# Three instead of two k-tile pairs of the first feed-forward product taken through seven block products, in another order of the pairs

## The chip, the core and the metric

The kernel runs on one core of a Trainium2 chip. The core has a matrix engine (TensorE, called PE in the profile), a vector engine (VectorE, DVE), a scalar engine (ScalarE, ACT), GpSimd (POOL) and SyncE (SP), which here issues all the transfers. Each engine takes its instructions in the order in which they stand in the program; engines wait for each other on semaphores. The metric is the device time of one execution in microseconds (us); lower is better.

## What is computed

The reference is a decoder layer in float32 for 256 tokens of width 2048: a gated mixer of two attention branches, a cross-attention, and a SwiGLU feed-forward block, each followed by a layer norm. The change lies in the first product of the feed-forward block, `x @ w_in`:

```python
D_MODEL = 2048
D_FF = -(-8 * D_MODEL // (3 * 256)) * 256      # 5632

def swiglu(x, w_in, w_out):
    g, u = jnp.split(x @ w_in, 2, axis=-1)
    return (jax.nn.silu(g) * u) @ w_out
...
        y = swiglu(x, w_ffn_in[l], w_ffn_out[l])
        x = layer_norm(ALPHA * x + y, ln_g[l, 2], ln_b[l, 2])
```

## The kernel before

Float32 products are made of three matmuls each. An operand is split into `hi` (rounded by ScalarE, L117) and `lo` (the rest, a subtraction on VectorE, L118), and `mm3` adds hi·hi (L268), hi·lo (L269) and lo·hi (L270) in PSUM. So every weight tile that comes from memory costs one activation, one subtraction, and then matmuls. L268 and L270 need only the `hi` half of the weight, L269 needs the `lo` half.

The feed-forward width 5632 is cut into 11 slices of 512 columns, j = 0 to 10. Slice 0 is made by the ordinary `product`. Slices 1 to 10 are ten **passes** of one loop. A pass makes the gate and the up columns of its slice for both halves of the tokens, so four accumulators of 128 tokens by 512 columns (x11, x12, x21, x22: token half, then gate or up). The depth 2048 is 16 k-tiles, taken as 8 pairs c = 0 to 7 (`KC = 2`). A pair can be done in two ways:

- `plain_cell`: for gate and for up one transfer of two weight tiles (512 KB) into a `raw` buffer, one split into an `hl` buffer (128 x 1024 elements), and 12 matmuls; 24 matmuls for the pair.
- `fast_cell`: gate and up times two k-tiles times two token halves form a 2 x 2 block product, done with seven block products instead of eight (Winograd's form of Strassen's scheme), 21 matmuls. The sums of activations it needs are made once ahead of the passes (`fast_acts`, tile `sq`). The sums of weights are made in each pass by VectorE: L914, L915 (tile `tw`), L918, L919 (tile `s`), 128 x 512 each, and then three splits of 128 x 1024 into `hl` and one of 128 x 512 into `s`. Four of the seven products go to PSUM banks of their own (m1, m5, m6, m7, pool `aux`). After the last fast pair of the pass, `sums` joins them into four `stage` tiles (L948 to L952).

At the end of a pass four VectorE additions read the accumulators (L990, L992), ScalarE applies silu (L991), a product is made (L993), and the result is written out to DRAM (`keep`, L196). `turn` reads it back with its tokens turned (four transfers, L181), VectorE transposes it (L187, four instructions), ScalarE and VectorE split it (L188, L190). That is done during the next pass.

Tile's scheduler decides the order of the instructions on each engine. There are five `raw` buffers, four `hl` buffers, one `tw` buffer, two `s` buffers, and 14 buffers `b8`, which hold among others the 4 quads of the input activations, `sq` and the turned results of the slices.

```python
    FAST = (0, 1)
    ORDER = (0, 2, 3, 1, 4, 5, 6, 7)
...
            for i, c in enumerate(ORDER):
                if c in FAST:
                    fast_cell(bk, x2T, sq, FAST.index(c), c, ws, c == FAST[-1])
```

Of the kernel before, what the change touches and what calls it, by code (L numbers as in the profile page):

```python
# [65 lines left out]
def trunk(ctx: ExitStack, tc: tile.TileContext, a, out: bass.AP):  # L66
# [34 lines left out]
    def stage(dtype=F32):  # L101
        return work.tile([P, W], dtype, tag="stage", name=nm("stage"), bufs=4)
# [55 lines left out]
    def to_quad(q, tt, src):  # L158
        p = ps_aux()
        for i in range(4):  # L160
            nc.tensor.transpose(p[:, i * P:(i + 1) * P], src[:, i * P:(i + 1) * P], ident)  # L161
        sl = slice(tt * P, (tt + 1) * P)
        pv = p.rearrange("p (k t) -> p k t", k=4)
        split(q.hi[:, :, sl], q.lo[:, :, sl], pv)
# [206 lines left out]
    for ps in wide(w_in[:, C_QI:C_KI], load_x):  # L371
        t = b8().rearrange("p (h t) -> p h t", h=8)
# [26 lines left out]
    for tt in range(NT):  # L399
# [8 lines left out]
        st = work.tile([P, 6], F32, tag="st1", name=nm("st1"))  # L408
# [448 lines left out]

    FAST = (0, 1)  # L860
    ORDER = (0, 2, 3, 1, 4, 5, 6, 7)

    def fast_acts():

        q = Quad()
        for t, c in enumerate(FAST):
            st = stage()
            a11, a12 = [tok[0][:, (2 * c + i) * P:(2 * c + i + 1) * P] for i in range(2)]
            a21, a22 = [tok[1][:, (2 * c + i) * P:(2 * c + i + 1) * P] for i in range(2)]
            s1, s2, s3, s4 = [st[:, i * P:(i + 1) * P] for i in range(4)]  # L870
            nc.vector.tensor_tensor(s1, a21, a22, op=ALU.add)
            nc.vector.tensor_tensor(s2, s1, a11, op=ALU.subtract)
            nc.vector.tensor_tensor(s3, a11, a21, op=ALU.subtract)
            nc.vector.tensor_tensor(s4, a12, s2, op=ALU.subtract)
            to_quad(q, t, st)
        return q

    class Banks:

# [78 lines left out]
    for j in range(DFF // W):  # L958
        gs = []

        def gate(tt, p):
            g = stage()
            nc.scalar.activation(g, p, AF.Silu)
            gs.append(g)

        q = Quad()
        d = spill()
        if j == 0:
            product(x2T, [wf[:, j * W:(j + 1) * W]], seq=8, stream_seq=3, done=gate)
            side.finish()  # L970
            sq = fast_acts()
            pu = product(x2T, [wf[:, DFF + j * W:DFF + (j + 1) * W]])
            for tt in range(NT):
                nc.vector.tensor_tensor(gs[tt], gs[tt], pu[tt], op=ALU.mult)
                keep(d, tt, gs[tt])
        else:
            ws = [wf[:, j * W:(j + 1) * W], wf[:, DFF + j * W:DFF + (j + 1) * W]]
            bk = Banks(None)
            for i, c in enumerate(ORDER):
                if c in FAST:  # L980
                    fast_cell(bk, x2T, sq, FAST.index(c), c, ws, c == FAST[-1])
                    flush()
                    side.step(1)
                    if c == FAST[-1]:
                        cs = sums(bk)
                else:
                    plain_cell(bk, x2T, c, ws, i == len(ORDER) - 1)
            for tt in range(NT):
                g, u = cs[2 * tt:2 * tt + 2]
                nc.vector.tensor_tensor(g, g, bk.t[f"x{tt + 1}1"], op=ALU.add)  # L990
                nc.scalar.activation(g, g, AF.Silu)  # L991
                nc.vector.tensor_tensor(u, u, bk.t[f"x{tt + 1}2"], op=ALU.add)  # L992
                nc.vector.tensor_tensor(g, g, u, op=ALU.mult)  # L993
                keep(d, tt, g)
        later.append(turn(q, d))
        q.mixed = True
        hT.append(q)
# [33 lines left out]
```

## Time and profile before

| what | value |
|---|---|
| median of 3 runs | 1470.9 us (1468.82 to 1473.25) |
| the profiled execution's own time | 1469.42 us |
| its span, first to last instruction | 1467.3 us |
| PE busy | 98% |
| DVE busy | 71% |
| ACT busy | 48% |
| granted TensorE clock | 0.998 of full speed |
| ten passes of the loop | from about 794 to about 1218 us of the span |

The busy shares are averages over the whole program. The change touches only the ten passes, a little under a third of the span, and what it is worth is read there: which engine has gaps, how long they are, and what ended them.

### The profile page before, as it was taken

What the parts mean: (1) busy time and instruction counts of PE and PEld (TensorE: products, weight loads), DVE (VectorE), ACT (ScalarE), POOL (GpSimd) and SP (SyncE); (2) the same over time, 40 slices, a digit from 0 to 9 for tenths busy, and PEclk for the clock granted to TensorE, in tenths of its full rate; (3) what the DMA queues carried; (4) which work ended last, traced back from release to release, by engine and by line L of the source; (5) the groups of instructions that cost most, each with busy time, mean ns of one, the idle gap of its engine ahead of it and who ended that gap; (6) DMA issues with size and microseconds to landing.
All of it is one profiled execution on the core that took longest, in us unless ns stands there. A gap on an engine that the chain in (4) does not pass through costs nothing.

```text
span 1467.3 us, 17933 instructions
## 1 busy us (share of the span) xinstructions
PE 1444.1 (98%) x6604; PEld 1198.4 (82%) x6604; DVE 1045.3 (71%) x1361; ACT 706.8 (48%) x830; POOL 19.6 (1%) x43
## 2 busy tenths in 40 slices
PE   8999999999999999999989999999999999999997
PEld 6988888888888888888868888888888888888885
DVE  6575986575756666986786888898888886544456
ACT  4554456454534444445644555555455454434341
POOL 0000000000000000000000000000000000000000
PEclk9999999999999999999999999999999999999999
DMA  9884667777667779968535666766776768666662
GB/s 284 194 270 144 198 210 228 227 236 225 214 202 231 219 254 316 231 185 272 177 131 182 206 222 218 242 214 216 229 223 222 243 206 265 191 198 190 197 216 100
DMA packets 197463, 316.60 MB, mean 216 GB/s; under 512 B 18688, under 2 KB 58752, under 8 KB 197376
## 3 DMA queue, kind: packets, MB, share of 16 engines
q1 hardware_dynamic: 197376, 315.47, 69.1%
q8 instruction: 51, 0.84, 0.2%
q14 instruction: 36, 0.29, 0.1%
HBM read 298.65 MB, written 16.78 MB: 215 GB/s over the span
## 4 chain that ended last, share of the span: by engine, by line
PE 91%; DMA 4%; DVE 3%; issue 1%; ACT 0%; POOL 0%; SPq 0%; POOLq 0%; DVEq 0%; ACTq 0%
PE acc L230 20%; PE acc L231 20%; PE acc L229 19%; PE acc L270 8%; PE acc L269 8%; PE acc L268 8%; PE aux L269 2%; PE aux L270 2%; PE aux L268 2%; DMA turn<-spill 1%; DMA raw<-in_w_in 1%; DVE b L751 1%; DVE hl L118 1%; DMA kvg<-in_kv_norm_g 1%; DMA spill<-stage 0%
## 5 line engine op out<-in xcount | busy, mean ns | idle before, releaser
L118 DVE TENSOR_TENSOR hl<-raw,hl 128x1024 fp32r<-128x1024 f32 (+2 forms) x475 | 571.1, 1212 | 272.3 <-ACT hl L117 271.3
L117 ACT ACTIVATE hl<-raw 128x1024 fp32r<-128x1024 f32 (+2 forms) x475 | 496.3, 1052 | 513.0 <-PE acc L231 347.2
L230 PE MATMUL acc<-hl,b 128*128 128x512 f32 (+1 forms) x1272 | 493.8, 388 | 0.7 <-DVE hl L118 0.5
L231 PE MATMUL acc<-hl,b 128*128 128x512 f32 (+1 forms) x1272 | 493.3, 388 | 0.0
L229 PE MATMUL acc<-hl,b 128*128 128x512 f32 (+1 forms) x1272 | 491.3, 389 | 0.7 <-ACT b L117 0.7
L230 PEld LDWEIGHTS acc<-hl,b 128*128 128x128 f32 x1272 | 238.9, 188 | 48.6 <-DVE hl L118 1.5
L229 PEld LDWEIGHTS acc<-hl,b 128*128 128x128 f32 x1272 | 238.8, 188 | 48.4 <-ACT b L117 0.9
L231 PEld LDWEIGHTS acc<-hl,b 128*128 128x128 f32 x1272 | 238.9, 188 | 48.1 <-DVE b L118 0.2
L269 PE MATMUL acc<-hl,b 128*128 128x512 f32 x584 | 227.8, 391 | 0.5 <-DVE hl L118 0.4
L270 PE MATMUL acc<-hl,b 128*128 128x512 f32 x584 | 226.9, 390 | 0.0
L268 PE MATMUL acc<-hl,b 128*128 128x512 f32 x584 | 210.3, 391 | 0.3 <-ACT hl L117 0.2
L269 PEld LDWEIGHTS acc<-hl,b 128*128 128x128 f32 x584 | 109.9, 188 | 25.1 <-DVE hl L118 2.2
L268 PEld LDWEIGHTS acc<-hl,b 128*128 128x128 f32 x584 | 110.0, 189 | 24.2 <-ACT hl L117 1.1
L270 PEld LDWEIGHTS acc<-hl,b 128*128 128x128 f32 x584 | 109.7, 188 | 22.7
L187 DVE STREAM_TRANSPOSE tr<-turn 128x256 f32<-128x256 f32 (+1 forms) x148 | 67.1, 511 | 64.2 <-DMA turn<-spill 64.1
L188 ACT ACTIVATE b<-tr 128x1024 fp32r<-128x1024 f32 (+1 forms) x37 | 37.4, 1014 | 76.9 <-DVE tr L187 75.3
L117 ACT ACTIVATE b<-aux 128x512 fp32r<-128x512 f32 (+1 forms) x50 | 26.7, 545 | 37.0 <-PE aux L161 21.5
L190 DVE TENSOR_TENSOR b<-tr,b 128x1024 fp32r<-128x1024 f32 (+1 forms) x37 | 42.8, 1162 | 1.8 <-ACT b L188 1.4
L117 ACT ACTIVATE hl<-s 128x1024 fp32r<-128x1024 f32 x20 | 21.3, 1063 | 31.0 <-DVE s L919 13.3
L914 DVE TENSOR_TENSOR tw<-raw,raw 128x512 f32<-128x512 f32 x20 | 13.8, 691 | 31.2 <-DMA raw<-in_w_ffn_in 31.1
L118 DVE TENSOR_TENSOR b<-aux,b 128x512 fp32r<-128x512 f32 (+1 forms) x50 | 30.0, 621 | 3.3 <-ACT b L117 3.0
L269 PE MATMUL aux<-hl,b 128*128 128x512 f32 x80 | 31.5, 394 | 0.1
(158 smaller groups left out, 1013.4 us busy)
## 6 DMA issues: line engine op xcount, KB each, us to landing
raw<-in_w_ffn_in SPq DMA_DIRECT2D x176, 512.0 KB, 4.8
raw<-in_w_in SPq DMA_DIRECT2D x143, 512.0 KB, 4.5
raw<-in_w_ffn_out SPq DMA_DIRECT2D x88, 512.0 KB, 4.2
raw<-in_w_out SPq DMA_DIRECT2D x32, 512.0 KB, 6.6
spill<-stage SPq DMA_DIRECT2D x56, 256.0 KB, 2.4
turn<-spill SPq DMA_DIRECT2D x104, 128.0 KB, 3.8
raw<-in_w_o_dsa SPq DMA_DIRECT2D x16, 512.0 KB, 4.6
raw<-in_w_o_moba SPq DMA_DIRECT2D x16, 512.0 KB, 4.0
```

Of the source, the lines that this page charges most:

```text
L117: nc.scalar.activation(hi, src, AF.Copy)
L118: return (eng or nc.vector).tensor_tensor(lo, src, f(hi), op=ALU.subtract)
L187: nc.vector.transpose(tr[:, i, :], v[:, i])
L188: nc.scalar.activation(hi, tr, AF.Copy)
L190: nc.vector.tensor_tensor(lo, tr, f(hi), op=ALU.subtract)
L229: nc.tensor.matmul(o[:, :n], xh, hi[:, kk, :n], start=k == 0, stop=False)
L230: nc.tensor.matmul(o[:, :n], xh, lo[:, kk, :n], start=False, stop=False)
L231: nc.tensor.matmul(o[:, :n], xl, hi[:, kk, :n], start=False, stop=k == kts - 1)
L268: nc.tensor.matmul(o, lh, rh, start=start, stop=False)
L269: nc.tensor.matmul(o, lh, rl, start=False, stop=False)
L270: nc.tensor.matmul(o, ll, rh, start=False, stop=stop)
L751: prev = nc.vector.scalar_tensor_tensor(t, t, scalar, self.rows[row][:, j * W:(j + 1) * W], op0=op0, op1=op1)
```

## The change

`FAST` gets a third pair, so in each pass three pairs go through `fast_cell` and five through `plain_cell`, and `ORDER` puts a plain pair behind each fast one: 0, 3, 1, 4, 2, 5, 6, 7, where it was 0, 2, 3, 1, 4, 5, 6, 7. `sums` runs after pair 2, the fifth in order, where it ran after pair 1, the fourth. `fast_acts` makes the sums of a third pair and needs a second quad, which takes one more of the `b8` buffers through all passes. Lines of the kernel move by two: L914 becomes L916, L919 becomes L921, L993 becomes L995, L187 and below stay.

```diff
-    FAST = (0, 1)
-    ORDER = (0, 2, 3, 1, 4, 5, 6, 7)
+    FAST = (0, 1, 2)
+    ORDER = (0, 3, 1, 4, 2, 5, 6, 7)
 
     def fast_acts():
 
-        q = Quad()
+        qs = []
         for t, c in enumerate(FAST):
+            if t % 2 == 0:
+                qs.append(Quad())
             st = stage()
...
-            to_quad(q, t, st)
-        return q
+            to_quad(qs[-1], t % 2, st)
+        return qs
...
                 if c in FAST:
-                    fast_cell(bk, x2T, sq, FAST.index(c), c, ws, c == FAST[-1])
+                    fast_cell(bk, x2T, sq[FAST.index(c) // 2], FAST.index(c) % 2, c, ws, c == FAST[-1])
```

The scheduler makes a new order of it. Three places on VectorE matter, all in the middle passes. **The first** is the start of a pass's work, from the last products of the pass before (L993) to the transposes of the turned result (L187). Before:

```order
L993 TENSOR_TENSOR stage_7972<-stage_7972,stage_7973 128x512
L993 TENSOR_TENSOR stage_7974<-stage_7974,stage_7975 128x512
L118 TENSOR_TENSOR hl_8186<-raw_8184,hl_8186 128x1024
L118 TENSOR_TENSOR hl_8209<-raw_8207,hl_8209 128x1024
L118 TENSOR_TENSOR hl_8228<-raw_8226,hl_8228 128x1024
L118 TENSOR_TENSOR hl_8245<-raw_8243,hl_8245 128x1024
L914 TENSOR_TENSOR tw_8268<-raw_8262,raw_8260 128x512
L915 TENSOR_TENSOR tw_8268<-raw_8262 128x512
L187 STREAM_TRANSPOSE tr_8201<-turn_8179 128x256 x4
```

And in the changed program (L995 is what L993 was):

```order
L995 TENSOR_TENSOR stage_8064<-stage_8064,stage_8065 128x512
L995 TENSOR_TENSOR stage_8066<-stage_8066,stage_8067 128x512
L118 TENSOR_TENSOR hl_8267<-raw_8265,hl_8267 128x1024
L921 TENSOR_TENSOR s_8296<-raw_8284,s_8296 128x512
L118 TENSOR_TENSOR hl_8288<-raw_8284,hl_8288 128x1024
L118 TENSOR_TENSOR s_8299<-raw_8286,s_8299 128x512
L118 TENSOR_TENSOR hl_8291<-tw_8292,hl_8291 128x1024
L118 TENSOR_TENSOR hl_8295<-s_8296,hl_8295 128x1024
L187 STREAM_TRANSPOSE tr_8259<-turn_8237 128x256 x4
```

Both have four rows of 128x1024 and two of 128x512 between L993 and L187; in the changed program they are the splits of the second fast pair, and the splits of the plain pair behind it stand behind L187. **The second place** follows. It is the last fast pair of the pass, up to the first plain split behind it. Before:

```order
L918 TENSOR_TENSOR s_8272<-raw_8262,tw_8268 128x512
L118 TENSOR_TENSOR hl_8264<-raw_8260,hl_8264 128x1024
L118 TENSOR_TENSOR s_8275<-raw_8262,s_8275 128x512
L919 TENSOR_TENSOR s_8272<-raw_8260,s_8272 128x512
L190 TENSOR_TENSOR b_1190_7796<-tr_8201,b_1190_7796 128x1024
L118 TENSOR_TENSOR hl_8267<-tw_8268,hl_8267 128x1024
L118 TENSOR_TENSOR hl_8271<-s_8272,hl_8271 128x1024
L118 TENSOR_TENSOR hl_8314<-raw_8312,hl_8314 128x1024
```

In the changed program, where it is the third fast pair:

```order
L118 TENSOR_TENSOR hl_8365<-raw_8361,hl_8365 128x1024
L920 TENSOR_TENSOR s_8373<-raw_8363,tw_8369 128x512
L118 TENSOR_TENSOR s_8376<-raw_8363,s_8376 128x512
L118 TENSOR_TENSOR hl_8368<-tw_8369,hl_8368 128x1024
L921 TENSOR_TENSOR s_8373<-raw_8361,s_8373 128x512
L118 TENSOR_TENSOR hl_8372<-s_8373,hl_8372 128x1024
L118 TENSOR_TENSOR hl_8415<-raw_8413,hl_8415 128x1024
```

Before, two rows of 128x1024 stand between the sum L919 and the split of its tile into `hl`; in the changed program the split follows the sum (L921) at once. **The third place** is later in the pass, ahead of the first fast pair of the next pass (L914, L916). Before:

```order
L118 TENSOR_TENSOR hl_8365<-raw_8363,hl_8365 128x1024
L951 TENSOR_TENSOR stage_8304<-stage_8304,aux_8155 128x512
L952 TENSOR_TENSOR stage_8306<-stage_8305,aux_8155 128x512
L118 TENSOR_TENSOR hl_8382<-raw_8380,hl_8382 128x1024
L118 TENSOR_TENSOR hl_8399<-raw_8397,hl_8399 128x1024
L914 TENSOR_TENSOR tw_8468<-raw_8462,raw_8460 128x512
```

In the changed program:

```order
L118 TENSOR_TENSOR hl_8449<-raw_8447,hl_8449 128x1024
L118 TENSOR_TENSOR hl_8466<-raw_8464,hl_8466 128x1024
L952 TENSOR_TENSOR stage_8406<-stage_8405,aux_8217 128x512
L118 TENSOR_TENSOR hl_8483<-raw_8481,hl_8483 128x1024
L953 TENSOR_TENSOR stage_8405<-stage_8405,aux_8213 128x512
L954 TENSOR_TENSOR stage_8407<-stage_8406,aux_8213 128x512
L916 TENSOR_TENSOR tw_8535<-raw_8529,raw_8527 128x512
```

The transfer into the second `raw` tile of L916 (raw_8529) takes the buffer of raw_8447, so it can be issued when the first row here is done; five rows stand between. Before, the second tile (raw_8462) takes the buffer of raw_8380, one row further from L914.

## Rows read from the trace of the kernel before

**Rows 1.** The page: busy time of each engine over the span.

```profile
PE 1444.1 (98%) x6604; PEld 1198.4 (82%) x6604; DVE 1045.3 (71%) x1361; ACT 706.8 (48%) x830; POOL 19.6 (1%) x43
```

**Rows 2.** Busy time by windows: two passes, from one L993 to the next.

```profile
core 0: us, PE busy (x) PEld busy (x) DVE busy (x) ACT busy (x) POOL busy (x), PEclk, DMA share, GB/s
1049.19:1091.43 42.24, 42.24 (x188) 34.91 (x187) 36.20 (x45) 22.21 (x25) 0.00 (x0) 1.00 0.69 224
1091.43:1133.67 42.24, 42.24 (x188) 34.91 (x187) 35.57 (x44) 21.27 (x24) 0.00 (x0) 1.00 0.71 224
```

**Rows 3.** Timeline of PE: first and last of 40 matmuls without a gap.

```profile
start us, us, engine line op out<-in xcount [idle before <-releaser]
1081.40 0.39 PE L270 MATMUL acc<-hl,b 128*128 128x512 f32 x1
...
1090.24 0.39 PE L270 MATMUL acc<-hl,b 128*128 128x512 f32 x1
```

**Rows 4.** Timeline of DVE: from L993 through the second fast pair.

```profile
1091.43 1.29 DVE L993 TENSOR_TENSOR stage<-stage,stage 128x512 f32<-128x512 f32 x2
1092.63 3.58 DVE L118 TENSOR_TENSOR hl<-raw,hl 128x1024 fp32r<-128x1024 f32 x3
1096.56 1.23 DVE L118 TENSOR_TENSOR hl<-raw,hl 128x1024 fp32r<-128x1024 f32 x1 [0.35 <-ACT hl L117]
1098.02 0.69 DVE L914 TENSOR_TENSOR tw<-raw,raw 128x512 f32<-128x512 f32 x1 [0.23 <-DMA raw<-in_w_ffn_in]
1098.63 0.69 DVE L915 TENSOR_TENSOR tw<-raw 128x512 f32<-128x512 f32 x1
1100.67 2.20 DVE L187 STREAM_TRANSPOSE tr<-turn 128x256 f32<-128x256 f32 x4 [1.36 <-DMA turn<-spill]
1102.79 0.66 DVE L918 TENSOR_TENSOR s<-raw,tw 128x512 f32<-128x512 f32 x1
1103.36 1.23 DVE L118 TENSOR_TENSOR hl<-raw,hl 128x1024 fp32r<-128x1024 f32 x1
1104.49 0.69 DVE L118 TENSOR_TENSOR s<-raw,s 128x512 fp32r<-128x512 f32 x1
1105.10 0.69 DVE L919 TENSOR_TENSOR s<-raw,s 128x512 f32<-128x512 f32 x1
1105.70 1.23 DVE L118 TENSOR_TENSOR hl<-tw,hl 128x1024 fp32r<-128x1024 f32 x1
1107.00 1.23 DVE L118 TENSOR_TENSOR hl<-s,hl 128x1024 fp32r<-128x1024 f32 x1
```

**Rows 5.** Timeline of SP at the same place: result out, turned result in.

```profile
1092.14 0.94 SPq L196 DMA_DIRECT2D spill<-stage  x2
1093.88 0.38 SPq L894 DMA_DIRECT2D raw<-in_w_ffn_in  x1
1094.91 1.80 SPq L181 DMA_DIRECT2D turn<-spill  x4
```

**Rows 6.** Timeline of DVE: the earliest pair of L993 and L187 that waits.

```profile
837.18 1.29 DVE L993 TENSOR_TENSOR stage<-stage,stage 128x512 f32<-128x512 f32 x2
...
847.74 2.18 DVE L187 STREAM_TRANSPOSE tr<-turn 128x256 f32<-128x256 f32 x4 [2.74 <-DMA turn<-spill]
```

**Rows 7.** Timeline of ACT: the split of the tile that L919 finishes.

```profile
1105.90 1.06 ACT L117 ACTIVATE hl<-s 128x1024 fp32r<-128x1024 f32 x1 [3.43 <-DVE s L919]
```

**Rows 8.** Timeline of DVE ahead of the next pass's first fast pair.

```profile
1073.89 1.23 DVE L118 TENSOR_TENSOR hl<-raw,hl 128x1024 fp32r<-128x1024 f32 x1
1075.44 1.23 DVE L118 TENSOR_TENSOR hl<-raw,hl 128x1024 fp32r<-128x1024 f32 x1 [0.32 <-ACT hl L117]
1080.02 0.69 DVE L914 TENSOR_TENSOR tw<-raw,raw 128x512 f32<-128x512 f32 x1 [3.35 <-DMA raw<-in_w_ffn_in]
```

**Rows 9.** Waits in all passes (790 to 1216 us): total us, times, longest.

```profile
DVE tw L914 <- DMA raw<-in_w_ffn_in: 31.1, 13, 4.2
DVE hl L118 <- ACT hl L117: 18.1, 31, 1.5
DVE tr L187 <- DMA turn<-spill: 14.8, 8, 2.7
PEld aux L269 <- DVE hl L118: 1.2, 3, 0.6
```

**Rows 10.** Groups by line, 770 to 800 us: the transposes of `fast_acts`.

```profile
L161 PE MATMUL aux<-ident,stage 128*128 128x128 f32 x8 | 1.4, 272 | 0.0
```

## Prediction

> **What bounds the kernel now.** I read the busy shares first [rows 1]: the matrix engine is busy 98% of the span, VectorE 71%. That is an average over stages, so the next view is the ten passes alone. Two of them, cut from one L993 to the next, last 42.24 us each [rows 2]. The reader should see two things there: the matrix engine has no gap in them, and VectorE is busy for 36.2 us of 42.24, far above its average.
>
> How full the matrix engine is must be read from starts, since its rows overlap. Forty matmuls start between 1081.40 and 1090.24 [rows 3], so one takes 8.84 / 39 = 0.2267 us. A pass has 2 fast pairs of 21 and 6 plain ones of 24, 186 matmuls, and 186 x 0.2267 = 42.2 us. That is the pass: the matrix engine sets its length. The list of waits agrees: it waited on VectorE for 1.2 us in all passes together, while VectorE waited 31.1 us for weights, 18.1 us for ScalarE and 14.8 us for the turned result [rows 9]. VectorE's waits cost nothing as long as the matrix engine has work.
>
> [...]
>
> **What the change removes.** Three matmuls per pass: 3 x 0.2267 = 0.68 us, 6.8 us over ten passes. The matrix engine's floor becomes 183 x 0.2267 = 41.5 us per pass.
>
> **What it adds.** Once: four transposes and one more split in `fast_acts`. Eight transposes took 1.4 us of the matrix engine [rows 10], so four cost 0.7 us; the vector work lies in slice 0, an ordinary product with little vector work, and I cost it at nothing (four short sums and a split, under 2 us if nothing covered them).
>
> In each pass a plain pair becomes a fast one. The price of a VectorE row is the distance to the next start where nothing waits: L118 on `s` at 1104.49, L919 at 1105.10, the next at 1105.70, so 0.605 us for 512 columns; L118 at 1103.36 to 1104.49, so 1.13 us for 1024 [rows 4]. A plain pair has two splits of 1024, 2.26 us. A fast one has five rows of 512 and three of 1024, 6.42 us. Added: 4.16 us per pass. ScalarE gets 1.5 us more on 22 busy us [rows 2] and stays far from the bound. No transfer of a pass is added: a fast pair loads the same two 512 KB tiles.
>
> The whole VectorE work of a new pass: 25 rows of 512 (15 of the fast pairs, 4 of `sums`, 6 of the end) at 0.605 = 15.1; 20 of 1024 (10 plain splits, 9 fast ones, L190) at 1.13 = 22.6; four transposes, 1100.67 to 1102.79, 2.1 [rows 4]. Sum 39.8 us. The same count for the pass before (20, 19 and 4) gives 35.7, against 36.2 busy in the window [rows 2], so the method holds.
>
> [...]
>
> So VectorE has 41.5 - 39.8 = 1.7 us per pass in which it may wait. Beyond that it sets the length. This is the step that decides: which of its waits are fixed by the order, and don't shrink when VectorE falls behind?
>
> **First, the turned result.** From the end of the second L993 (VectorE is free at 1092.63) to the first L187 (1100.67) pass 8.04 us [rows 4]. That is the way through memory: the results go out, the turned read starts at 1094.91 [rows 5] and lands when L187 starts. VectorE cannot shorten it, since the clock starts at its own L993. The longest case in the loop is 837.18 + 1.2 to 847.74, 9.4 us [rows 6]. In the changed order the rows between are again four of 1024 and two of 512, 5.73 us, and the next row is L187. So VectorE stands still for 8.04 - 5.73 = 2.3 us there, and the splits of the next plain pair are queued behind it; the matrix engine, through with the second fast pair, waits for them. Before, the same 2.3 us were there (0.35 + 0.23 + 1.36 marked, the rest in short gaps), but VectorE had 6 us to spare. The weight transfer that SP issues between result and turned read waits for the first split behind L995, as it did before [rows 5], so I leave 8.04.
>
> **Second, the last sum of the third fast pair.** Its split stands directly behind it. L919 started at 1105.10, ScalarE could take its tile at 1105.90 for 1.06 us [rows 7], and the subtraction came at 1107.00 [rows 4]: 1.90 us from start to start. Before, a row of 1024 filled most of it. Now only the 0.6 us of L921 itself does: 1.3 us of wait.
>
> **Third, the weights of the next first fast pair.** Their second tile can be fetched when the split of raw_8447 is done. Before, from the end of that buffer's split (1073.89 + 1.23) to L914 at 1080.02 passed 4.9 us [rows 8]. Five rows stand between now, 2 x 1.13 + 3 x 0.605 = 4.1 us, so about 0.9 us of wait (the split's end lies 0.1 behind the next start). Before, the wait was 3.35 there [rows 8]; it shrinks because VectorE is later, not to nothing.
>
> Length of a full new pass: 39.8 + 2.3 + 1.3 + 0.9 = **44.3 us**, 2.1 more than 42.24. The bounds: not under 39.8 + 2.3 = 42.1 if the last two waits vanish in others, and at the other end 46.5 with the 9.4 us of [rows 6] and 0.8 more at the weights.
>
> Not all passes are full. In the changed order five are (slices 2 to 6): 10.5 us; in one of them only four rows follow the freed weight buffer, 0.6 more. In slices 7 and 8 L190 is put off (no `b8` buffer is free; `sq` holds one more): 43.2, so +1.0 each, again 0.6 more in one: 2.6. Slice 1 has no sum directly ahead of its split: 44.3 - 1.3 = 43.0, +0.8. Slice 9 has neither L187 nor L190; VectorE has 36.6 us, and the matrix engine's floor holds: -0.7. Slice 10 gets the postponed L187 and L190; two of these stand ahead of its last fast pair's splits, some 1 us of wait against the floor: +0.3. With the transposes: 10.5 + 0.6 + 2.6 + 0.8 - 0.7 + 0.3 + 0.7 = 14.8 us.
>
> The profiled execution took 1469.42 us (span 1467.3), 1.5 below the median of the runs. 1469.4 + 14.8 = 1484.2; the median lies by as much above as before at most, and I say 1485.
>
> **The rivals.**
>
> - *The matrix engine still sets the pass: faster.* It gains 6.8 - 0.7 = 6.1, so 1463.3. For this VectorE's waits must fit into 1.7 us per pass; the way of the result through memory would have to be under 7.4 us instead of 8.04. For it speaks that 39.8 is under 41.5; against it, that none of the passes with a wait had under 8.0. Chance 0.07.
> - *Only the turned result's wait stays* and the others are hidden behind it, since VectorE catches up where the matrix engine is held: a full pass of 42.1 to 43, others at the floor of 41.5: 1469.4 - 2 to + 6, so 1467 to 1475. Chance 0.19.
> - *More waits than I count.* The late splits hold `hl` buffers, ScalarE waits for these, and the weights come later still: 46.5 us and more per pass, 1469.4 + 10 x 2.5 to 10 x 4, so 1495 to 1509. For it speaks that the changed stretch alternates fast and plain with four `hl` buffers; against it, that I find the buffers free in time when I follow them through the order. Chance 0.10.
> - *Each VectorE row costs its whole duration.* 43.9 + 4.5 = 48.4, +6.2 per pass, about 1520. The starts in [rows 4] speak against it. By the durations in the same rows it is 25 x 0.69 + 20 x 1.23 + 2.1 = 43.9. Chance 0.02. [...]
>
> **How the numbers follow.** My forecast, VectorE sets the pace with these three waits, has 0.62 and gives 1479 to 1491. About 0.3%, 4.4 us, is what a measurement of this kernel can tell from no change. Slower: 0.62 + 0.12 + a sixth of the second rival = 0.77; within: the rest of it, 0.16; faster 0.07. The range that leaves out no more than 2 in 10 reaches into the second rival and to the start of the third: 1470 to 1495.
>
> **What will show it.** In the changed profile the middle passes last 44 us instead of 42.24, the matrix engine has gaps in them that end on L118 of VectorE, and VectorE's own waits in each are the turned result (2.3), ScalarE on `s` (1.3) and weights (about 1). The slice without L187 lasts 41.5. If the gaps of the matrix engine are absent, or VectorE's waits sum to less than 1.7 per pass, I am wrong.

## The result, and the profile after

The changed kernel takes 1512.8 us (median of 4 runs, 1511.25 to 1513.72), the kernel before on the same chip 1470.8. The ratio is 1.0282, with a 95% interval of 1.0267 to 1.0297: slower, as forecast, but by 42 us where I had said 14, and outside the range of 1470 to 1495.

The page after answers to [rows 1]: VectorE is busier and the matrix engine less, which now has gaps.

```profile
PE 1456.3 (96%) x6578; PEld 1199.9 (79%) x6578; DVE 1085.4 (72%) x1426; ACT 721.2 (48%) x851; POOL 19.1 (1%) x43
```

The windows view, cut from one product L995 (the L993 of before) to the next, answers to [rows 2]. The columns are length, then busy time and number of instructions of PE, weight loads, DVE, ACT and POOL, then the granted clock, the share of the DMA engines and GB/s.

```profile
839.57:888.43 48.86, 45.22 (x190) 36.25 (x189) 40.21 (x50) 24.73 (x28) 0.00 (x0) 0.97 0.63 194
...
982.38:1028.20 45.82, 43.53 (x188) 34.88 (x188) 40.03 (x51) 24.38 (x27) 0.00 (x0) 1.00 0.64 207
1028.20:1075.50 47.30, 43.91 (x184) 35.22 (x183) 40.03 (x50) 23.76 (x26) 0.00 (x0) 0.96 0.63 200
...
1169.87:1214.14 44.27, 43.01 (x188) 34.83 (x187) 37.12 (x45) 22.93 (x27) 0.00 (x0) 1.00 0.65 214
1214.14:1261.69 47.55, 40.70 (x162) 32.20 (x163) 39.26 (x47) 23.18 (x26) 0.00 (x0) 0.93 0.64 211
sum 422.12, PE 389.76 PEld 312.37 DVE 355.01 ACT 210.86 POOL 0.00; mean PE 43.31 PEld 34.71 DVE 39.45 ACT 23.43 POOL 0.00
```

The same nine stretches of the kernel before sum to 380.59 us, so 41.5 of the 43.7 us by which the spans differ (1511.0 against 1467.3) lie here. VectorE's work in a full pass is 40.0 us, as counted ahead (39.8). The pass is not 44.3 us long but 46 to 49.

Where does the pass stand still? The timeline of VectorE from the results to the transposes (L187) and on answers to [rows 4]. Lines left out are marked with three dots; the three rows with a wait longer than 1 us are all that this pass has.

```profile
1028.20 1.28 DVE L995 TENSOR_TENSOR stage<-stage,stage 128x512 f32<-128x512 f32 x2
...
1034.02 1.21 DVE L118 TENSOR_TENSOR hl<-s,hl 128x1024 fp32r<-128x1024 f32 x1
1038.92 2.16 DVE L187 STREAM_TRANSPOSE tr<-turn 128x256 f32<-128x256 f32 x4 [3.69 <-DMA turn<-spill]
1041.00 2.32 DVE L118 TENSOR_TENSOR hl<-raw,hl 128x1024 fp32r<-128x1024 f32 x2
...
1051.90 1.22 DVE L118 TENSOR_TENSOR hl<-s,hl 128x1024 fp32r<-128x1024 f32 x1 [2.17 <-ACT hl L117]
...
1062.61 0.69 DVE L916 TENSOR_TENSOR tw<-raw,raw 128x512 f32<-128x512 f32 x1 [1.41 <-DMA raw<-in_w_ffn_in]
```

The matrix engine at the same place:

```profile
1038.22 0.84 PE L268 MATMUL acc<-hl,b 128*128 128x512 f32 x3
1042.24 0.50 PE L269 MATMUL acc<-hl,b 128*128 128x512 f32 x1 [3.18 <-DVE hl L118]
...
1043.79 0.63 PE L270 MATMUL acc<-hl,b 128*128 128x512 f32 x1
1044.22 0.63 PE L268 MATMUL acc<-hl,b 128*128 128x512 f32 x1
...
1046.78 0.53 PE L270 MATMUL acc<-hl,b 128*128 128x512 f32 x1
1047.15 0.39 PE L268 MATMUL acc<-hl,b 128*128 128x512 f32 x1
```

The reader should follow one chain here. VectorE has nothing to do from 1035.23 (1038.92 - 3.69), since the next thing in its row is the transposes and the turned result isn't there. The split that the matrix engine needs next stands behind the transposes. The matrix engine had 3.83 us of matmuls ready (its gap begins at 1042.24 - 3.18 = 1039.06); the wait, the transposes and the split together take 7.0 us (1035.23 to 1042.24). The rest, 3.18 us, is its gap. Soon after, the starts of the matmuls from 1043.79 to 1047.15 lie 0.42 us apart, eight times, instead of 0.2267 [rows 3]. The windows view has the granted clock at 0.50 there:

```profile
1043.66:1047.07 3.41, 3.41 (x10) 2.62 (x9) 3.41 (x5) 1.06 (x1) 0.00 (x0) 0.50 0.82 277
```

That is another 1.55 us. 41.5 + 3.18 + 1.55 = 46.2 of the 47.3 us; the rest lies in gaps of under 0.5.

Why the turned result is late, SyncE shows, against [rows 5]:

```profile
1028.31 0.37 SPq L896 DMA_DIRECT2D raw<-in_w_ffn_in  x1
1028.91 0.95 SPq L196 DMA_DIRECT2D spill<-stage  x2
1030.65 0.38 SPq L896 DMA_DIRECT2D raw<-in_w_ffn_in  x1
1033.91 1.80 SPq L181 DMA_DIRECT2D turn<-spill  x4
```

A weight transfer of 512 KB now goes out 0.6 us ahead of the results. The turned read, which waits for both results to have landed, follows 5.0 us after them instead of 2.8 (1092.14 to 1094.91 before). In the passes the results land 3.0 to 5.2 us after issue, where they took 2.0 to 2.6. The list of waits over all passes answers to [rows 9]; before, the matrix engine waited 1.2 us on VectorE, and VectorE 14.8 for the turned result. The first two rows tell of the same stops, once at the weight load and once at the matmul.

```profile
PEld acc L269 <- DVE hl L118: 36.0, 14, 4.2
PE acc L269 <- DVE hl L118: 30.0, 12, 3.7
DVE tr L187 <- DMA turn<-spill: 28.3, 8, 4.5
DVE tw L916 <- DMA raw<-in_w_ffn_in: 25.5, 15, 4.9
```

### The profile page after: what moved, and what is told of

Its sections match the earlier page's. It is cut to its first block, busy times and chain, and to the rows that moved or that the text cites. A ratio compares the mean times of both kernels' runs of the same rounds, so it can differ in the third digit from the quotient of the medians.

```text
span 1511.0 us, 17954 instructions
## 1 busy us (share of the span) xinstructions
PE 1456.3 (96%) x6578; PEld 1199.9 (79%) x6578; DVE 1085.4 (72%) x1426; ACT 721.2 (48%) x851; POOL 19.1 (1%) x43
## 5 line engine op out<-in xcount | busy, mean ns | idle before, releaser
L118 DVE TENSOR_TENSOR hl<-raw,hl 128x1024 fp32r<-128x1024 f32 (+2 forms) x465 | 558.5, 1210 | 261.4 <-ACT hl L117 260.7
L117 ACT ACTIVATE hl<-raw 128x1024 fp32r<-128x1024 f32 (+2 forms) x465 | 483.4, 1050 | 471.4 <-PE acc L231 348.5
L231 PEld LDWEIGHTS acc<-hl,b 128*128 128x128 f32 x1272 | 238.8, 188 | 48.2 <-DVE b L118 0.2
L229 PEld LDWEIGHTS acc<-hl,b 128*128 128x128 f32 x1272 | 238.8, 188 | 48.1 <-ACT b L117 0.9
L230 PEld LDWEIGHTS acc<-hl,b 128*128 128x128 f32 x1272 | 238.9, 188 | 47.7 <-DVE hl L118 0.6
L269 PE MATMUL acc<-hl,b 128*128 128x512 f32 x524 | 210.4, 402 | 30.6 <-DVE hl L118 30.3
L270 PE MATMUL acc<-hl,b 128*128 128x512 f32 x524 | 208.4, 399 | 0.0
L268 PE MATMUL acc<-hl,b 128*128 128x512 f32 x524 | 186.0, 400 | 1.1 <-ACT hl L117 1.1
L269 PEld LDWEIGHTS acc<-hl,b 128*128 128x128 f32 x524 | 101.2, 193 | 58.9 <-DVE hl L118 37.7
L187 DVE STREAM_TRANSPOSE tr<-turn 128x256 f32<-128x256 f32 (+1 forms) x148 | 66.9, 511 | 80.6 <-DMA turn<-spill 80.6
L268 PEld LDWEIGHTS acc<-hl,b 128*128 128x128 f32 x524 | 101.4, 194 | 26.2 <-ACT hl L117 4.0
L270 PEld LDWEIGHTS acc<-hl,b 128*128 128x128 f32 x524 | 101.0, 193 | 21.1
L117 ACT ACTIVATE hl<-s 128x1024 fp32r<-128x1024 f32 x30 | 31.8, 1061 | 64.9 <-DVE s L921 39.5
L269 PE MATMUL aux<-hl,b 128*128 128x512 f32 x120 | 47.5, 396 | 1.2 <-DVE hl L118 1.2
L270 PE MATMUL aux<-hl,b 128*128 128x512 f32 x120 | 46.8, 390 | 0.0
L268 PE MATMUL aux<-hl,b 128*128 128x512 f32 x120 | 44.4, 407 | 0.6 <-ACT hl L117 0.6
L118 DVE TENSOR_TENSOR hl<-s,hl 128x1024 fp32r<-128x1024 f32 x30 | 36.6, 1218 | 11.7 <-ACT hl L117 11.5
L117 ACT ACTIVATE hl<-tw 128x1024 fp32r<-128x1024 f32 x30 | 31.8, 1059 | 27.3 <-PE acc L270 11.3
```

The source lines that it names most:

```text
L117: nc.scalar.activation(hi, src, AF.Copy)
L118: return (eng or nc.vector).tensor_tensor(lo, src, f(hi), op=ALU.subtract)
L187: nc.vector.transpose(tr[:, i, :], v[:, i])
L229: nc.tensor.matmul(o[:, :n], xh, hi[:, kk, :n], start=k == 0, stop=False)
L230: nc.tensor.matmul(o[:, :n], xh, lo[:, kk, :n], start=False, stop=False)
L231: nc.tensor.matmul(o[:, :n], xl, hi[:, kk, :n], start=False, stop=k == kts - 1)
```

## The experiments

The theory when these began: VectorE sets the pace, as forecast, and its waits are longer than I sized them. The rivals were that each VectorE row costs its whole duration, and that the order of the pairs is the harm, not the third fast pair. All runs were compared with the kernel before on the same chip.

**Order alone.** Two fast pairs as before, in the changed order.

```diff
     FAST = (0, 1)
-    ORDER = (0, 2, 3, 1, 4, 5, 6, 7)
+    ORDER = (0, 3, 1, 4, 2, 5, 6, 7)
```

> Two fast pairs as before the change, but visited in the changed order. If VectorE's load is what the change costs: its work is back at 35.7 us of a pass and the matrix engine's 186 matmuls take 42.2, so VectorE may wait 6.5 us per pass; the waits seen after the change (3.7 + 2.2 + 1.4) just about fit, so a pass lasts 42.2 to 43 and the time is 1469 to 1480. If the order of the pairs is itself the harm (the transfer ahead of the results, the split right behind the sums), passes of 44 us and more, over 1485.

Measured: 1503.8 us, ratio 1.0226 (1.0204 to 1.0248). The order alone costs 33 of the 42 us. Its windows, from one L993 to the next, its timeline of VectorE, and of the matrix engine:

```profile
985.01:1032.41 47.40, 43.35 (x183) 35.42 (x184) 36.17 (x44) 22.05 (x25) 0.00 (x0) 0.96 0.62 199
1032.41:1078.68 46.27, 42.74 (x181) 34.91 (x181) 36.15 (x45) 21.31 (x24) 0.00 (x0) 0.96 0.64 205
```

```profile
1043.73 2.16 DVE L187 STREAM_TRANSPOSE tr<-turn 128x256 f32<-128x256 f32 x4 [4.29 <-DMA turn<-spill]
1045.81 2.32 DVE L118 TENSOR_TENSOR hl<-raw,hl 128x1024 fp32r<-128x1024 f32 x2
```

```profile
1047.05 0.79 PE L269 MATMUL acc<-hl,b 128*128 128x512 f32 x1 [3.52 <-DVE hl L118]
```

VectorE has 36.2 us of work, as before the change, and 10 us of room in a pass, and the pass is nearly as long as with three fast pairs. So neither VectorE's work nor the price of its rows sets the pass; the same gap behind L187 does. Over the nine stretches the passes are 29.1 us longer than before (409.73 against 380.59); the gaps over 0.3 us sum to 22.6, and four passes at the clock of 0.96 add about 1.7 each (eight matmuls take 3.52 us from start to start there instead of 1.81).

With this the theory fell, and I formed another, the **lead**: VectorE can be ahead of the matrix engine only by the split tiles that are held, and a fast pair's tile is worth fewer matmuls than a plain one's; where the transposes come at the end of a short lead, the matrix engine stops.

**The way of the results.** In `spill_first` the weight transfer seen above is held until both results are issued. In `old_spill` and `order_alone_old` the turned read doesn't wait for this pass's results at all: it reads those of the pass before, so these kernels leave out the right data of the second product.

```diff
 # spill_first, in plain_cell
-            raw = load_chunk(w, c)
+            raw = load_chunk(w, c, after=kept[-1] if c == 4 and n == 1 and kept else None)
 # old_spill (on the changed kernel), order_alone_old (on order_alone)
-        later.append(turn(q, d))
+        later.append(turn(q, olds[-1] if olds else d))
+        olds.append(d)
```

> One weight transfer of 512 KB (the up half of the second plain pair) is issued behind the two results of the pass instead of ahead of them. Theory: the results then land 2 us after issue instead of 4.4, the wait for the turned result falls from 3.7 to 2.3 us, the matrix engine's gap there stays short enough that its clock doesn't fall, and the wait behind the last sum falls from 2.2 to 1.3: 1.4 + about 0.5 to 0.9 less in eight passes, 1494 to 1500. Rival, VectorE's rows cost their whole duration: 1508 or more. Rival, the transfer that is now late makes VectorE wait for weights instead: 1508 to 1516 with the wait for weights up by 1.4 us per pass.

> The turned read of each slice reads the results of the slice before, which are long in memory, so nothing waits for the way through memory (what the second product multiplies is other data; the number and size of all transfers stay). Theory: the 3.7 us of wait go, and with them the fall of the clock and its 0.9 us: passes of 42.5 us, and 8 x 4.5 = 36 us less, 1475 to 1482; bounds 1472 (all passes at the matrix engine's floor) and 1490 (another wait takes half). Rival, VectorE's rows cost their whole duration: 1505 or more.

> Two fast pairs in the changed order, as order_alone, but the turned read takes the results of the slice before (what the second product multiplies is other data; transfers stay the same), so that VectorE doesn't stand before the transposes. Theory (the lead): the wait of 4 us stood where only a fast pair's splits were ahead; without it the passes go back to 42.2 to 43: 1468 to 1478. Rival, late weights in the changed order: 1490 or more, with VectorE's waits for weights above 30 us in all passes.

Measured: `spill_first` 1504.6 (1.0238, 1.0215 to 1.0261), half of what was expected. The results land faster (2.0 to 2.7 us after issue in the first seven passes, 3.0 to 4.4 in the changed kernel), but only every other pass gains: there the turned result comes 8.6 to 8.9 us after the results and VectorE waits under 1 us for it; in the passes between it comes after 9.3 to 12.7 us. What was won on the way out is lost on the way back: the turned read takes 4.2 to 8.9 us to land, 2.7 to 4.4 in the changed kernel. `order_alone_old` 1473.1 (1.0023, 1.0011 to 1.0034), as expected: without the wait for the turned result the order costs only 3 us, with passes of 42 to 44 us. The edit does two things, though: the transposes, which no longer wait, also move to a place between the two products (L994 there), so the run doesn't part the wait from the place. `old_spill` 1496.2 (1.0186, 1.0145 to 1.0226), which missed: with three fast pairs, 26 us stay even so. Two rows of it show what comes next (the profiled execution took 1504.9 us):

```profile
992.96 0.69 DVE L916 TENSOR_TENSOR tw<-raw,raw 128x512 f32<-128x512 f32 x1 [2.42 <-DMA raw<-in_w_ffn_in]
1000.78 1.23 DVE L118 TENSOR_TENSOR hl<-s,hl 128x1024 fp32r<-128x1024 f32 x1 [1.31 <-ACT hl L117]
```

Here VectorE waits behind the last sum, as forecast, and for weights (41.1 us in all passes, 25.5 in the changed kernel), but these are the weights of the third fast pair, where the forecast had no wait. Some of the loss may be the edit's own: the transposes moved between the additions and the products, and put the results off by their 2 us. So a loss with three fast pairs is left when the wait for the turned result is gone, and 33 + 26 us is more than the 42 of the change: the two are no plain sum. That one wait hides in the other would explain it, and isn't shown.

**The place of the transposes in VectorE's row, and the number of split tiles.** `later_turn3` moves one split of the next plain pair ahead of the transposes (L190 then comes one split later, too). `hl5` has a fifth `hl` tile, which, besides, moves the transposes three sums later. `hl5_order_alone` and `hl5_before` are the same on two fast pairs in the changed order, and on the kernel before. `raw6` has a sixth weight tile.

```diff
 # later_turn3, in turned(), for the slices of the feed-forward product (hold=3)
+        for _ in range(hold):
+            yield
 # hl5, hl5_order_alone, hl5_before (three places); bias 3 -> 1, NTURN 2 -> 1 make room
-        t = stream.tile([P, D], F32R, tag="hl", name=nm("hl"), bufs=4)
+        t = stream.tile([P, D], F32R, tag="hl", name=nm("hl"), bufs=5)
 # raw6 (four places); bias 3 -> 1 makes room
-        raw = stream.tile([P, KC, W], F32, tag="raw", name=nm("raw"), bufs=5)
+        raw = stream.tile([P, KC, W], F32, tag="raw", name=nm("raw"), bufs=6)
```

> The changed kernel with five hl tiles instead of four; the room comes from one bias and one turn tile instead of three and two. Theory (the lead): VectorE can be ahead of the matrix engine by no more than the split tiles that are held; a plain pair's tile is worth 12 matmuls, 2.72 us, a fast pair's 7, 1.59 us, so in the stretch fast, plain, fast, plain, fast the lead runs out however little VectorE has to do in the rest of the pass. One tile more adds up to 2.7 us of lead: passes of 43 to 44.5 instead of 47, 1475 to 1490. Rival, the work of VectorE over the whole pass plus fixed waits sets the length: 1505 to 1515. Rival, late weights set it: 1505 to 1515, since there are no more raw tiles.

> The changed kernel with six raw tiles instead of five (the room comes from one bias tile instead of three), so that each weight transfer can start one tile earlier. Theory (the lead of the split tiles): the waits for weights go (1.4 us of a pass) but VectorE still has its debt at the transposes: 1498 to 1512. Rival, late weights are what the order costs: 1470 to 1485.

> The changed kernel with one split of the next plain pair moved from behind the four transposes to ahead of them on VectorE; nothing else. Theory (the lead): the matrix engine's gap of 3.2 us per pass stands because that split is queued behind the wait for the turned result; its tile is 2.72 us of matmuls, so the gap shrinks to under 1 us, passes of 44 to 45, 1484 to 1496. Rival, VectorE's work and its waits add up whatever their order: the wait shrinks by the split's 1.1 us at most, 1500 to 1514.

> The kernel before with five hl tiles, one bias and one turn tile: the control for hl5. The matrix engine has no gap in its passes there, so one more tile can give nothing: 1467 to 1474, passes of 42.24. If it is 1465 or less, hl5 gained from something other than the passes of the first feed-forward product; if it is over 1476, the smaller bias and turn pools cost something that hl5 paid too.

> Two fast pairs in the changed order with five hl tiles: hl5 without its third fast pair. If the lead was what the order lacked: from 1503.8 to 1468 to 1474, as hl5_before; then the third fast pair costs 1 to 7 us more than its three matmuls per pass give (hl5 has 1475). If the third pair pays once the lead is there: 1476 to 1482.

Measured: `later_turn3` 1498.4 (1.0190, 1.0172 to 1.0208), 14 us less for one row in another place, though just over what the lead theory expected. `hl5` 1475.0 (1.0027, 1.0015 to 1.0040), as the lead theory had it. `raw6` 1492.2 (1.0155, 1.0110 to 1.0201), better than that theory allowed. `hl5_before` 1467.4 (0.9978, 0.9970 to 0.9987): its passes are the 42.24 us of before, so the smaller pools cost nothing there; its 2 us lie outside them, 1.27 ahead of the first L993 and 0.75 behind the last. It is the fastest kernel of this study. But `hl5_order_alone` has 1504.6 (1.0222, 1.0205 to 1.0240), where the theory said 1468 to 1474: a fifth tile does nothing for the changed order as such, and the lead as I had counted it is not the cause. VectorE in `hl5` first, then in `hl5_order_alone`, from the results to the transposes:

```profile
1059.94 1.29 DVE L995 TENSOR_TENSOR stage<-stage,stage 128x512 f32<-128x512 f32 x2
...
1067.34 0.69 DVE L916 TENSOR_TENSOR tw<-raw,raw 128x512 f32<-128x512 f32 x1 [0.97 <-DVE hl L118]
1067.95 0.69 DVE L917 TENSOR_TENSOR tw<-raw 128x512 f32<-128x512 f32 x1
1068.55 0.69 DVE L920 TENSOR_TENSOR s<-raw,tw 128x512 f32<-128x512 f32 x1
1070.50 2.17 DVE L187 STREAM_TRANSPOSE tr<-turn 128x256 f32<-128x256 f32 x4 [1.26 <-DMA turn<-spill]
```

```profile
1029.65 1.29 DVE L993 TENSOR_TENSOR stage<-stage,stage 128x512 f32<-128x512 f32 x2
...
1034.87 1.22 DVE L118 TENSOR_TENSOR hl<-raw,hl 128x1024 fp32r<-128x1024 f32 x1
1041.11 2.15 DVE L187 STREAM_TRANSPOSE tr<-turn 128x256 f32<-128x256 f32 x4 [5.02 <-DMA turn<-spill]
```

The turned result comes 9 to 10 us after the results in both. In `hl5` VectorE spends 8 of them on rows that stand ahead of the transposes; in `hl5_order_alone` it has 5.2 us of rows and stands still for 5. What `hl5` gained came together with the place of the transposes. That the place did it, and not the tile, is argued: no run moves the transposes by these three sums with four tiles. For it speaks that the tile alone gave nothing in `hl5_order_alone`, nor in another order of three fast pairs (1486.1 us for `third_spread` with four tiles, 1487.3 for `hl5_spread` with five, both below). `raw6` shows the other half: its transposes wait only 1.2 to 2.1 us, but the matmuls ready then last 1.5 to 3.4 us, and its gaps are as long as ever. (The rows are of its slowest execution, 1503.9 us; the other three took 1488.5 to 1494.3.)

**Plain pairs between all fast ones.** Three fast pairs in other orders; `spread_late_old` with the edit of `old_spill`, `hl5_spread` with that of `hl5`.

```diff
-    ORDER = (0, 3, 1, 4, 2, 5, 6, 7)
+    ORDER = (0, 3, 4, 1, 5, 2, 6, 7)   # third_spread, hl5_spread
+    ORDER = (0, 3, 4, 1, 5, 6, 2, 7)   # spread_late, spread_late_old
```

> Three fast pairs, two plain pairs between the first and the second (0, 3, 4, 1, 5, 2, 6, 7). If waits that the order fixes make up the 47 us of a pass, another order moves it: between 1495 and 1520, and VectorE's waits have other sizes by the same sum (39.8 + waits = pass). If VectorE's rows cost their whole duration, the pass stays at 47 and the time within 1508 to 1516 with the sum of waits unchanged.

> Three fast pairs in the order (0, 3, 4, 1, 5, 6, 2, 7): two plain pairs between any two fast ones. Theory (the lead): VectorE falls behind by 1.7 us in each fast pair (6.4 of its own against 4.76 of matmuls) and by some 9 at the results and transposes, and regains 3.2 in each plain one; its largest debt is 7.2 us here, 7.8 in third_spread, 9.8 in the changed kernel. So passes of 42 to 43 and 1472 to 1484. Rival, VectorE's work over the pass and fixed waits: the same work, 39.8, so 1486 to 1512 whatever the order.

> Five hl tiles and the order (0, 3, 4, 1, 5, 2, 6, 7): largest debt 7.8 us instead of 9.8, one tile more of lead, and the transposes stand behind splits of plain pairs. Passes at the matrix engine's floor of 41.5 to 42.2 where the weights come in time: 1464 to 1470. If the weights don't (five raw tiles, two of them held by each fast pair), 1472 to 1480.

> The order (0, 3, 4, 1, 5, 6, 2, 7) with the turned read of each slice taking the results of the slice before (what the second product multiplies is other data). If spread_late lost its 20 us to the turned result, which landed 10.9 us after the results: passes of 42 to 43, 1466 to 1480. If it lost them to weights or to VectorE's work in the fast pairs: 1488 to 1500.

Measured: `third_spread` 1486.1 (1.0109, 1.0091 to 1.0127), under both ranges that were expected: the same work of VectorE (40.1 us in a pass), 27 us less. One of its passes, from one L994 (the additions ahead of the products) to the next:

```profile
1016.45:1059.46 43.01, 43.01 (x190) 35.20 (x189) 40.08 (x51) 23.38 (x27) 0.00 (x0) 1.00 0.70 220
```

Cut like this, five of its nine stretches have 42.6 to 43.2 us, so a length of 47 was never forced by VectorE's work. `spread_late` 1498.7 (1.0182, 1.0159 to 1.0205) and `hl5_spread` 1487.3 (1.0116, 1.0100 to 1.0131) both missed what the lead theory gave, by 15 us and by 7 or more; `spread_late` lies in its rival's range. The debt that I had counted from pair to pair left out where the results go: in these two, two weight transfers go out between the first result and the turned read (one before the change), which lands 10 to 12 us after the results in `spread_late` and, in the worse passes, 12 to 13 in `hl5_spread`. In `spread_late`:

```profile
1038.70 0.69 DVE L921 TENSOR_TENSOR s<-raw,s 128x512 f32<-128x512 f32 x1
1043.87 2.16 DVE L187 STREAM_TRANSPOSE tr<-turn 128x256 f32<-128x256 f32 x4 [4.48 <-DMA turn<-spill]
1045.96 1.18 DVE L118 TENSOR_TENSOR hl<-s,hl 128x1024 fp32r<-128x1024 f32 x1
```

`spread_late_old`, without that wait, has 1481.6 (1.0086, 1.0066 to 1.0107), 17 us less and just over what was expected.

**Put together.** Five tiles or a spread order, with the results ahead of a weight transfer. `hl5_spill`, `spread_late_spill`, `hl5_late_spill` and `hl5_spread_spill` hold the transfer that `spill_first` holds; `hl5_late_spill` and `hl5_late_spill2` have the order of `spread_late` and five tiles, and the last holds another one:

```diff
 # hl5_late_spill2
-            raw = load_chunk(w, c)
+            raw = load_chunk(w, c, after=kept[-1] if c == 5 and n == 0 and kept else None)
```

> hl5 (the changed kernel with five hl tiles) and the results issued ahead of the weight transfer as in spill_first. The gap of 1.2 to 2.7 us per pass that hl5 keeps behind the transposes should go, since the results land earlier: passes of 42 to 43, 1464 to 1472. If the weight transfer that is now later costs as much again, 1474 to 1480.

> The order (0, 3, 4, 1, 5, 6, 2, 7), four hl tiles, and both results issued ahead of the weight transfer of the second plain pair; the transposes then stand ahead of the second fast pair's own splits. If the late landing of the results was spread_late's loss: the turned result comes 8 us after the results, a wait of 2 to 3 us, 1474 to 1488. If the place of the transposes ahead of a fast pair's splits matters as much: 1490 to 1500.

> Order (0, 3, 4, 1, 5, 6, 2, 7), five hl tiles, results ahead of the weight transfer: all that the lead theory asks for. Passes at or near the matrix engine's floor of 41.5: 1460 to 1467, under the kernel before (1469.6). If weights or VectorE's work in a fast pair still hold the matrix engine, 1468 to 1476 with passes of 42.3 and more.

> Order (0, 3, 4, 1, 5, 2, 6, 7) with five hl tiles, as hl5_spread, and the results ahead of the weight transfer. If hl5_spread lost 15 us to the turned result (12.5 us after the results there): the turned result comes after 8 to 9 us and 1465 to 1475. If not, 1480 or more.

> Order (0, 3, 4, 1, 5, 6, 2, 7), five hl tiles, and the results ahead of the transfer that went out just before them (pair 5's gate half), so that no other transfer is held back. If the lead and the landing of the results are the whole loss: passes of 41.5 to 42.3, 1460 to 1468. If the transposes stand too near to the second fast pair's last split, which the matrix engine needs next: a gap of 1 to 2 us per pass stays, 1474 to 1486.

Measured: `hl5_spill` 1472.2 (1.0019, 1.0010 to 1.0029), the best with three fast pairs. Its transposes stand 10.7 us and more behind the results, VectorE doesn't wait for them in the middle passes, and these last 42.4 to 42.8 us:

```profile
1011.75:1054.15 42.40, 42.19 (x184) 34.12 (x183) 40.04 (x50) 23.54 (x26) 0.00 (x0) 1.00 0.71 223
```

`spread_late_spill` 1527.7 (1.0408, 1.0379 to 1.0437), `hl5_late_spill` 1522.8 (1.0369, 1.0345 to 1.0392) and `hl5_spread_spill` 1512.1 (1.0290, 1.0270 to 1.0311) are among the slowest of all, and say nothing on the question: in those orders the transfer that is held would have gone out long before, and SyncE stood still with all that came behind it. `spread_late_spill` on SyncE, with a stop of 11.3 us:

```profile
1019.84 9.94 SPq L899 DMA_DIRECT2D raw<-in_w_ffn_in  x4
1041.08 2.08 SPq L196 DMA_DIRECT2D spill<-stage  x2
```

From 1029.78 to 1041.08 no transfer is issued (the longest such stop in the middle passes of `spread_late` is 7.4 us), and VectorE then waits 5.59 us for the split of that tile. `hl5_late_spill2`, which holds the right one, has 1495.9 (1.0153, 1.0132 to 1.0175), still a miss: the wait for the turned result is 1.3 to 4.0 us, and another gap of 2.22 us opens elsewhere, where pairs 2, 7 and 0 follow each other and VectorE waits 3.5 us for weights.

**All of it in one table**, from the timelines of the first seven stretches (eight with two fast pairs): rows of VectorE between the results and the transposes, the wait there, and the matrix engine's gap behind it. (0 means none over 0.25 us.)

| kernel | rows ahead, us | wait, us | gap, us | time, us |
|---|---|---|---|---|
| before | 6.3 to 6.6 | 1.4 to 2.7 | 0 | 1470.8 |
| changed | 5.75 | 3.1 to 4.5 | 1.7 to 3.7 | 1512.8 |
| order_alone | 5.7 to 6.0 | 3.1 to 5.1 | 2.0 to 3.9 | 1503.8 |
| hl5_order_alone | 5.15 | 4.1 to 5.2 | 1.8 to 3.1 | 1504.6 |
| spread_late | 6.4 to 6.5 | 3.6 to 5.6 | 2.2 to 3.9 | 1498.7 |
| later_turn3 | 6.9 to 8.5 | 1.0 to 3.0 | 0 in five, 1.0, 2.4 | 1498.4 |
| raw6 | 7.9 to 10.0 | 1.2 to 2.1 | 2.1 to 4.1 | 1492.2 |
| hl5 | 7.8 to 9.0 | 0.2 to 1.8 | 0 in two, 0.9 to 2.7 | 1475.0 |
| hl5_spill | 10.7 to 12.7 | 0, once 0.8 | 0.6 or less | 1472.2 |

(The rows ahead include other waits, as for weights, above all in `raw6` and `hl5_spill`. The first three columns are of one execution, the last is the median: the profiled execution of `raw6` took 12 us more than its median, that of `later_turn3` 4 less, the others lie within 3.)

## Why the prediction was right in sign and wrong in size

- **The removed matmuls and VectorE's added work** were sized rightly: 183 matmuls fit into the passes of 42.4 us in `hl5_spill`, and VectorE is busy for 40.0 us of a full pass, where I had said 39.8.
- **The three waits** stand where they were put. In the pass from 1028.20 each is longer than forecast:

| term of a full pass | forecast, us | measured, us |
|---|---|---|
| VectorE's work | 39.8 | 40.0 |
| turned result | 2.3 | 3.7 |
| split behind the last sum | 1.3 | 2.2 |
| next weights | 0.9 | 1.4 |
| pass | 44.3 | 47.3 |

Over the first seven stretches only the turned result is too small in all (3.1 to 4.5). The split behind the last sum has 1.2 us in four of them and 2.2 in three, the longest wait for weights goes from under 0.9 to 2.6.

- **"I leave 8.04"** is a step that failed. The weight transfer between result and turned read does stay where it was; I had not seen that another one now stands just ahead of the results. The way through memory takes 8.9 to 10.2 us instead, and 2.3 becomes 3.1 to 4.5. Holding this one transfer back (`spill_first`) is worth 8 us of the time.
- **The step that failed most** is the one I called deciding: that VectorE has 1.7 us per pass in which it may wait, and that before, the same wait cost nothing because "VectorE had 6 us to spare". `order_alone` has those 6 us, and loses 33 us of time. What covers a wait in VectorE's row is not its spare time over the pass, but the matmuls that are ready when the wait begins: 3.0 to 4.8 us in the changed kernel, 3.6 to 5.5 in `order_alone`. Before, they lasted from 1099.31 (the start of the wait [rows 4]) to 1106.60, 7.3 us. There 48 matmuls of two plain pairs start from 1095.27 on. The second fast pair opens at 1106.15, and its first matmul that needs the split behind L187 (L269) starts at 1106.60, 2.0 us after that split was done (1104.59):

```profile
1106.15 0.39 PE L268 MATMUL aux<-hl,b 128*128 128x512 f32 x1
1106.37 0.39 PE L268 MATMUL acc<-hl,b 128*128 128x512 f32 x1
1106.60 0.39 PE L269 MATMUL aux<-hl,b 128*128 128x512 f32 x1
```

So I charged the fast pair for a loss that lies mostly in the order (33 of the 42 us): the result comes later, and the transposes stand where fewer matmuls are ready. The count of VectorE's work gave the right sign for a reason that covers a part only. So the sign was in part luck: by the same count the order alone would have cost nothing.
- **The clock** was not in the sum: 1.55 us in the pass above. In the three passes with 0.96 (from 888.43, 935.53 and 1028.20) the slow matmuls also make the first bank of `sums` late, ScalarE copies it late, and the split that stands behind the copy is late: the wait behind the last sum is 2.2 us. With the same row of ScalarE in the pass from 982.38 (gap 1.66 us, clock 1.00) it is 1.18, and where ScalarE copies the bank later it is 1.2 at either clock. Of the gaps behind the transposes in the first seven passes of the changed kernel five, of 3.18 to 3.73 us, come with a lower clock (0.93 to 0.97 over the pass), the ones of 1.66 and 3.25 us don't (1.00); in `spread_late` matmuls 0.43 us apart come behind a gap of 2.17 us (1092.18), and after 2.76 us in `hl5_order_alone` the matmuls go on at 0.23 us. So the length of the gap alone doesn't decide it; what does isn't shown.
- **The slices at the end** were wrong too: slice 9, forecast at the floor of 41.5, has 44.27, and the stretch behind it 47.55; VectorE waits for weights there (up to 4.9 us in the list of waits).
- **The rivals.** "Each VectorE row costs its whole duration" gave 1520, near the result, and is wrong: `order_alone` takes 4.2 us of rows out of a pass and gains 9 us in all, and `third_spread` does the same rows in passes of 42.6 to 43.2 us. "More waits than I count" (1495 to 1509) came nearest in kind, but that the `hl` buffers made them isn't borne out: a fifth gave nothing in `order_alone` and in the order of `third_spread`, and took 38 us off the changed kernel only together with another place of the transposes. The first two rivals fall with passes of 46 to 49 us.
- **What stays open.** `old_spill` loses 26 us without the turned result's wait, perhaps part of it by its own edit. I can't divide the changed kernel's 42 us between the order and the third pair more finely than 33 for the order alone: three fast pairs in the order of before were not run, so what the third pair costs by itself isn't known. Even where the wait for the turned result is gone, the third fast pair pays nothing in any version here: 1472.2 (`hl5_spill`) against 1467.4 for two fast pairs with the same five tiles. A middle pass of `hl5_spill` has 42.4 us, 0.9 over the matrix engine's floor, and nearly all of it lies in one place: from 1029.74 to 1031.97 six matmuls take 2.23 us from start to start instead of 1.36. That is the last sum again (L924 there), whose tile ScalarE gets late, with the next plain split queued behind it:

```profile
1029.02 1.06 ACT L117 ACTIVATE hl<-s 128x1024 fp32r<-128x1024 f32 x1 [1.33 <-DVE s L924]
1030.14 0.50 PE L268 MATMUL aux<-hl,b 128*128 128x512 f32 x1
1031.08 0.50 PE L268 MATMUL acc<-hl,b 128*128 128x512 f32 x1 [0.21 <-ACT hl L117]
```

These 0.9 us are more than the 0.68 that the three removed matmuls save.

## What to carry to other kernels

In this kernel an engine that serves another in order had to be judged at its longest stop, not by its sum over the loop: find the row that waits, add what stands between it and the next thing the other engine needs, and subtract the work that is ready at that moment. When an order changes, follow each queue past the place where a result leaves and comes back, the transfers just ahead of it included; here one transfer and one split in another place were worth 8 and 14 us. Test the order and the new work apart first: the run with the old work in the new order told more than all sums.

## What the runs showed that I had not expected

- A hold on one transfer stopped SyncE's whole queue: the edit that gained 8 us in the changed order left SyncE idle for 11.3 us of a pass in another, and the time went up by 29 us (1498.7 to 1527.7).
- Five split tiles instead of four leave two fast pairs in the changed order where they were (1503.8 and 1504.6), and take 38 us off three; with the fifth tile the scheduler put three short sums ahead of the transposes there.
- The matrix engine's lower clock doesn't always begin with the gap: behind the one of 3.18 us in the changed kernel six matmuls still start 0.23 to 0.34 us apart, then eight 0.42 apart; behind the one of 3.52 us in `order_alone` the first is slow already (0.59 us to the next start, then 0.43); and behind one of 3.25 us in the changed kernel (1089.64) none is (0.22 to 0.34 apart).
